# Conditioning rows in PSUM, a narrower first stage and twice the load buffers in a diffusion layer

## The chip, the cores and the metric

The kernel runs on one core of a Trainium2 chip. The metric is the device time of one execution, in microseconds (us). The kernel before took 854.05 us (median of 3 runs, 852.78 to 855.21). Lower is better.

## The reference, cut to what matters

One layer of a diffusion backbone over 512 latent tokens with 256 context tokens, all in float32, width 1024:

```python
mod   = silu(c) @ w_ada + b_ada          # six vectors of 1024: sh1, sc1, g1, sh2, sc2, g2
mod_c = silu(c_ctx) @ w_ada + b_ada      # the same for the context; only sh1c, sc1c are used
uc = layer_norm(ctx) * (1 + sc1c) + sh1c
kvc = uc @ w_in[:, :KV_COLS]             # context keys and values -> start states of the scans
u = layer_norm(x) * (1 + sc1) + sh1
k, v, q, g, p_in, gate_a, gate_b = split(u @ w_in)
ret  = retention(q, k, v, g, states) @ w_branch_ret     # 8 heads, forward and backward, swish gate g
pool = pool_mixer(p_in) @ w_branch_pool                 # means over windows of 2, 4, 8, 16
mix  = (sigmoid(gate_a) * ret + sigmoid(gate_b) * pool) @ w_out
x = layer_norm(ALPHA * x + g1 * mix) * ln1_g + ln1_b
u2 = layer_norm(x) * (1 + sc2) + sh2
x = layer_norm(ALPHA * x + g2 * conv_ffn(u2)) * ln2_g + ln2_b
```

`conv_ffn` is an up-projection to 2 x 2816, a 3x3 depthwise convolution, gelu times gate and a down-projection.

## The kernel before, in words

Every large product is done in three passes of 128x512 matmuls on operands that are split in a rounded high part and the rest: hi x hi, hi x lo, lo x hi. `split` (L84) makes the two parts of a weight tile: ScalarE (ACT) casts `raw` to `hi` (L88), and GpSimd (POOL) or VectorE (DVE) subtracts to get `lo` (`sub`, L83). The tiles `hi` and `lo` have two buffers each, the landing tile `raw` has three (L63). PSUM has eight banks, handed out by `bank()`.

The latent tokens lie feature-major: 8 tiles kt of 128 features x 512 tokens (`xnT`, after the norm and a transpose). The first stage goes over kt = 0 to 7. For each kt it loads two blocks of `w_ada` (512 KB each; `wst`) and one of `w_first` (`first_load`), the columns of q (4 tiles of 128) and of the first N_G0 = 4 swish gate tiles. `first_mod` gets the shift and the scale of this kt: `matvec` (L201) multiplies a 128x1024 block by `silu_c`, a row that stands in SBUF on all partitions (made by `silu_row`, L107), and sums along the row, and `finish_mod` (L204) adds the bias, for a scale also the 1. `modulate` (L212) then forms `uh` (ACT, L214) and, by way of `u` (ACT, L217), `ul` (POOL, L83). TensorE (PE) multiplies: `g0_mm` (L334) does hi, lo and ul passes for the four q tiles and then for the four gate tiles, which fill all eight banks over the whole stage. From kt = 4 on, `ctx_mod` (L222) makes the same shift and scale for the context, two blocks per kt, with `silu_cc` in SBUF (L225).

After it come steps of one weight tile each (`step`, `run_steps`, L171): step i first preloads and splits the weights of step i + 1 (`prep`), then multiplies and does what its `post` says. In this order: four gate steps `g_step` for the other four gate tiles (with q's copies from PSUM, L410, the statistics, transposes and modulation of the context, and the rest of `ctx_mod`), the pool step `p_step(0)`, four key steps (`kv_steps`), `p_step(1)`, eight value steps with `p_step(2)` and `p_step(3)` among them, then eight steps each for the two branch gates, during which the retention is done, and the two branch projections (L742, L754). Each key and value step also loads three more 512 KB blocks of `w_ada` by way of `raw` and multiplies them on DVE (`ada_tiles`). The table of decays (`decay_tables`) is made in the first key step: ACT does 16 exponentials of 128x128 (L559, L560) in a row.

What sets the order: within `ordered(*ORDS)` all engines do their instructions in the order of the code. The first stage stands in such a region. After it the kernel calls `ordered(*ORD0)`, which keeps only PE, SP (the queue that issues all DMAs) and DVE in the order of the code, and from the first key step on only SP is kept; what isn't kept is put in order by a scheduler that works with times of its own. The output projection (L804 on), the up-projection with its convolution (L1020 on) and the down-projection follow.

Of the kernel before, what the change touches and what calls it, by code (L numbers as in the profile page):

```python
# [9 lines left out]
F32 = mybir.dt.float32  # L10
# [19 lines left out]
ALPHA = 2.0 ** 0.25  # L30
N_G0 = 4
N_FRONT = 18
# [13 lines left out]
def layer_kernel(ctx: ExitStack, tc: tile.TileContext, a: dict):  # L46
# [16 lines left out]
    def raw4(shape=(P, D)):  # L63
        return sb.tile(list(shape), F32, tag="raw", bufs=3, name=nm("raw"))

    def row():
        return sb.tile([P, D], F32, tag="row", bufs=3, name=nm("row"))
# [33 lines left out]
    mod = keep("mod", [P, 48])  # L101
    modc = keep("modc", [P, 16])
    neg_half = keep("neg_half", [P, 1])
    dve.memset(neg_half, -0.5)
    keep("gap0", [P, 24])

    def silu_row(cols):  # L107

        t = row()
        for hf in range(2):  # L110
            ps = bank()
            for j in range(4):
                k = 4 * hf + j
                pe.transpose(ps[:, j * P:(j + 1) * P], cols[:, k:k + 1].broadcast_to([P, P]), ident)
            act.copy(t[:, hf * SEQ:(hf + 1) * SEQ], ps)
        return t

# [85 lines left out]

    def finish_mod(m, j, scale):  # L204
        dve.tensor_scalar(m[:, j:j + 1], m[:, j:j + 1], bada[:, j:j + 1], 1.0 if scale else 0.0, ALU.add, ALU.add)

# [15 lines left out]
    def ctx_mod(kt):  # L222
        for j in (kt, 8 + kt):
            w = ada_slot(j)
            dve.scalar_tensor_tensor(w, w, 1.0, silu_cc, ALU.mult, ALU.mult, accum_out=modc[:, j:j + 1])  # L225
            finish_mod(modc, j, j >= 8)

# [13 lines left out]
    def first_load(kt):  # L241
        for j in (kt, 8 + kt):
            load(ada_slot(j), a["wada"][j])
        return load(raw4((P, NF0)), a["w_first"][kt])

    def first_mod(kt):
        for j in (kt, 8 + kt):
            matvec(j, ada_slot(j), junk)
            finish_mod(mod, j, j >= 8)

# [44 lines left out]
    dve.tensor_tensor(cols[:, 1], cols[:, 0], cols[:, 1], ALU.mult)  # L295
    silu_c = silu_row(cols[:, 1])
    x_stats(1)
# [13 lines left out]
    held = [x_trans(0, 1)]  # L311
    matvec(0, ada_slot(0), junk)
    x_norm(3, dve, lo_half)
# [4 lines left out]
    warm(N_W)  # L318
    finish_mod(mod, 0, False)
    matvec(8, ada_slot(8), junk)  # L320
    finish_mod(mod, 8, True)
    wh, wl = (sb.tile([P, NF0], F32R, tag=t, bufs=2, name=nm(t)) for t in ("hi", "lo"))
    act.activation(uh[:, 0, :], xnT[:, 0, :], AF.Identity, bias=mod[:, 0:1], scale=mod[:, 8:9])
    for cs, cp in ((lo_half, dve.tensor_copy), (hi_half, act.copy)):
        cp(wh[:, cs], raw0[:, cs])
        sub(pool, wl[:, cs], raw0[:, cs], wh[:, cs].bitcast(F32))
# [14 lines left out]
    for kt in range(NKT):  # L341
        wh, wl = ready
        if kt == 0:
            g0 = [bank() for _ in range(4)]
            g0_mm(kt, range(0, 4), range(2))
            held += [x_trans(2, 1), x_trans(3, 1)]
            g0_mm(kt, range(0, 4), range(2, 3))
            for h in held:
                act.copy(*h)
            g0 += [bank() for _ in range(N_G0)]  # L350
            ready = split(first_load(1), (P, NF0), pool)
            first_mod(1)
            modulate(mod, 1, 9, xnT[:, 1, :], uh[:, 1, :], ul[:, 1, :], pool)
        elif kt + 1 < NKT:
            ready = first_prep(kt + 1, first_load(kt + 1))
        if kt:
            g0_mm(kt, range(0, 4))
        g0_mm(kt, range(4, 4 + N_G0))
        if kt == 1:
            silu_cc = load(row(), a["c_ctx"].broadcast_to([P, D]))  # L360
        elif kt == 2:
            for hf in range(2):
                cs = slice(hf * SEQ, (hf + 1) * SEQ)
                t = t2()
                act.activation(t, silu_cc[:, cs], AF.Sigmoid)
                dve.tensor_tensor(silu_cc[:, cs], silu_cc[:, cs], t, ALU.mult)
# [29 lines left out]

    def ctx_trans():
        for tb in range(2):
            transpose_tb(put_ctxT, ctx_raw[:, tb, :], tb)

    def ctx_modulate():
        for kt in range(NKT):
            modulate(modc, kt, 8 + kt, ctx_nT[:, kt, :], uch[:, kt, :], ucl[:, kt, :], pool,
                     act if kt % 2 else dve)

    def g_step(h):
        def post(ps):
            if h == N_G0:
                for f in range(4):
                    act.activation(qT[:, f, :], g0[f], AF.Copy, scale=DK ** -0.5)  # L410
                for f in range(2):
# [3 lines left out]
                for tb, (mu, rs) in enumerate(ctx_stats):
                    dve.tensor_scalar(ctx_raw[:, tb, :], ctx_raw[:, tb, :], mu, rs, ALU.subtract, ALU.mult)
            elif h == N_G0 + 1:
                for f in range(2, N_G0):
                    put_g(f, g0[4 + f])
                ctx_mod(h)  # L420
            elif h == N_G0 + 2:
                ctx_trans()
                ctx_mod(h)
# [107 lines left out]
    def decay_tables():  # L531
# [29 lines left out]
        for g in range(2):
            t = t2((P, 4, P))
            for j in range(4):
                h = 4 * g + j
                dve.tensor_scalar(t[:, j, :], grids[:, 0, :], lgf[:, h:h + 1], None, ALU.mult)
                dve.scalar_tensor_tensor(t[:, j, :], grids[:, 1, :], lgb[:, h:h + 1], t[:, j, :], ALU.mult, ALU.add)
            act.activation(t, t, AF.Exp)
            dve.tensor_tensor(kv[2][:, 4 * g:4 * g + 4, :], t, ident.unsqueeze(1).broadcast_to([P, 4, P]), ALU.add)

# [677 lines left out]
```

## Time and profile before

| what | value |
|---|---|
| median of 3 runs | 854.05 us |
| the profiled execution, its own time | 853.42 us |
| its span, first to last instruction | 851.6 us |
| PE busy | 810.9 us (95%) |
| DVE, POOL, ACT busy | 568.0, 422.1, 360.6 us |
| mean granted clock of PE | 0.99 |
| moved by DMA | 106.94 MB |

PE is busy for 95% of the span, so what can be had lies in the 41 us in which it isn't, and in the few stretches with a lower granted clock. The page's slices show where they are: at the start, in slices 2 to 4, 6 and 9 of 40 (the first stage and the key and value steps), around the output projection, and behind PE's last matmul.

### The profile page before, as it was taken

How to read it: one execution, taken by the hardware profiler on the slowest of the kernel's cores; microseconds unless marked ns; L12 is line 12 of the kernel's file. 1: busy time of each engine (PE TensorE's matmuls, PEld its weight loads, DVE VectorE, ACT ScalarE, POOL GpSimd, SP SyncE). 2: the span in 40 equal slices, each digit the busy share in tenths (PEclk: the TensorE clock that was granted, in tenths of full speed). 3: DMA queues.
4: the chain of work that ended last, by engine and by line, in shares of the span. 5: the costliest groups of instructions: out<-in, count | busy, mean ns of one | idle time of the engine just before them, and what ended most of it. 6: DMA issues, size and time to landing. Idle time of an engine off the chain costs nothing.

```text
span 851.6 us, 10522 instructions
## 1 busy us (share of the span) xinstructions
PE 810.9 (95%) x3865; PEld 673.7 (79%) x3865; DVE 568.0 (67%) x967; ACT 360.6 (42%) x574; POOL 422.1 (50%) x301
## 2 busy tenths in 40 slices
PE   6988999989999999999899899999999999999993
PEld 4767877868788888888687898888888888888883
DVE  7899996777247774253756759888877777512148
ACT  4434636131354323233414557666666666223200
POOL 4876420303353213022633768988888888211245
PEclk9999999999999999999999999999999999999997
DMA  9932357677311103234613511332222323333202
GB/s 353 347 120 76 124 197 237 212 246 239 104 50 50 50 25 125 99 124 163 205 64 123 174 38 64 123 99 94 93 90 97 100 99 99 108 111 130 73 1 99
DMA packets 33780, 106.94 MB, mean 126 GB/s; under 512 B 4528, under 2 KB 5312, under 8 KB 33728
## 3 DMA queue, kind: packets, MB, share of 16 engines
q1 hardware_dynamic: 33728, 106.27, 36.7%
q8 instruction: 30, 0.49, 0.2%
q14 instruction: 22, 0.18, 0.1%
HBM read 104.14 MB, written 2.11 MB: 125 GB/s over the span
## 4 chain that ended last, share of the span: by engine, by line
PE 43%; DVE 3%; POOL 2%; ACT 1%; issue 1%; POOLq 0%; DVEq 0%
PE ps L95 14%; PE ps L94 14%; PE ps L93 14%; POOL S L83 1%; ACT t L871 1%; DVE S L1140 1%; DVE S L1149 1%; DVE S L835 1%; DVE sm L836 0%; POOL sm L123 0%; DVE xr L848 0%; DVE t L1135 0%; POOL sm L122 0%; POOL S L1147 0%; POOL S L1117 0%
## 5 line engine op out<-in xcount | busy, mean ns | idle before, releaser
L95 PE MATMUL ps<-S,lo 128*128 128x512 f32 (+1 forms) x544 | 210.3, 388 | 5.0 <-POOL lo L83 2.6
L93 PE MATMUL ps<-S,hi 128*128 128x512 f32 (+1 forms) x544 | 211.4, 389 | 2.6 <-ACT hi L88 2.6
L94 PE MATMUL ps<-S,hi 128*128 128x512 f32 (+1 forms) x544 | 210.6, 387 | 0.0
L83 POOL TENSOR_TENSOR lo<-raw,hi 128x1024 fp32r<-128x1024 f32 (+1 forms) x63 | 147.7, 2346 | 124.0 <-ACT hi L88 112.9
L965 DVE SCALAR_TENSOR_TENSOR t<-ps,convw,t 128x441 f32<-128x441 f32 (+1 forms) x258 | 163.8, 691 | 45.7 <-POOL t L963 45.5
L88 ACT CAST hi<-raw 128x1024 fp32r<-128x1024 f32 (+1 forms) x98 | 99.4, 1014 | 161.8 <-PE ps L94 52.3
L95 PEld LDWEIGHTS ps<-S,lo 128*128 128x128 f32 x544 | 102.7, 189 | 27.5 <-POOL lo L83 3.5
L93 PEld LDWEIGHTS ps<-S,hi 128*128 128x128 f32 x544 | 102.2, 188 | 23.4 <-ACT hi L88 3.0
L963 POOL TENSOR_TENSOR t<-t,t 128x448 f32<-128x448 f32 x88 | 101.9, 1158 | 36.0 <-ACT t L1046 32.5
L94 PEld LDWEIGHTS ps<-S,hi 128*128 128x128 f32 x544 | 102.4, 188 | 20.3
L94 PE MATMUL ps<-S,S 128*128 128x512 f32 (+1 forms) x308 | 112.2, 364 | 0.0
L95 PE MATMUL ps<-S,S 128*128 128x512 f32 (+1 forms) x308 | 112.2, 364 | 0.0
L93 PE MATMUL ps<-S,S 128*128 128x512 f32 (+1 forms) x308 | 111.4, 365 | 0.0
L83 DVE TENSOR_TENSOR lo<-raw,hi 128x1024 fp32r<-128x1024 f32 x37 | 51.0, 1379 | 49.4 <-ACT hi L88 49.3
L94 PE MATMUL ps<-lo,S 128*128 128x512 f32 x208 | 81.3, 391 | 0.9 <-DVE lo L83 0.9
L95 PE MATMUL ps<-hi,S 128*128 128x512 f32 x208 | 80.8, 389 | 0.0
L83 POOL TENSOR_TENSOR S<-raw,S 128x1024 fp32r<-128x1024 f32 x21 | 50.4, 2402 | 59.9 <-ACT S L734 44.4
L93 PE MATMUL ps<-hi,S 128*128 128x512 f32 x208 | 77.5, 391 | 0.0
L1043 ACT ACTIVATE t<-ps,convb,convw 128x512 f32<-128x512 f32 x43 | 33.6, 780 | 76.2 <-PE ps L95 76.2
L93 PEld LDWEIGHTS ps<-S,S 128*128 128x128 f32 x308 | 58.1, 189 | 9.2
L95 PEld LDWEIGHTS ps<-S,S 128*128 128x128 f32 x308 | 58.1, 189 | 9.2
L94 PEld LDWEIGHTS ps<-S,S 128*128 128x128 f32 x308 | 58.1, 189 | 9.1
(208 smaller groups left out, 1130.2 us busy)
## 6 DMA issues: line engine op xcount, KB each, us to landing
raw<-in_w_up SPq DMA_DIRECT2D x44, 512.0 KB, 3.3
raw<-in_wada SPq DMA_DIRECT2D x32, 512.0 KB, 4.0
raw<-in_w_down SPq DMA_DIRECT2D x22, 512.0 KB, 3.3
S<-in_wada SPq DMA_DIRECT2D x16, 512.0 KB, 6.8
raw<-in_w_first SPq DMA_DIRECT2D x8, 512.0 KB, 7.7
raw<-in_w_v SPq DMA_DIRECT2D x16, 256.0 KB, 3.0
raw<-in_w_ga SPq DMA_DIRECT2D x8, 512.0 KB, 3.4
raw<-in_w_gb SPq DMA_DIRECT2D x8, 512.0 KB, 3.3
```

The lines of the kernel that those rows point to most:

```text
L83: eng.tensor_tensor(out, x, y, ALU.subtract)
L88: act.copy(hi, raw)
L93: pe.matmul(out, lhsT=sh, rhs=mh, start=first, stop=False)
L94: pe.matmul(out, lhsT=sh, rhs=ml, start=False, stop=False)
L95: pe.matmul(out, lhsT=sl, rhs=mh, start=False, stop=last)
L835: dve.scalar_tensor_tensor(z, ps, rs, lnb[:, cs], ALU.mult, ALU.add)
L871: act.activation(u[:, j, :], ps[:, js], AF.Identity, bias=sh, scale=sc)
L963: pool.tensor_tensor(o, o, i, ALU.add)
L965: dve.scalar_tensor_tensor(o, i, w, o, ALU.mult, ALU.add)
L1043: act.activation(acc, src, AF.Identity, bias=convb[:, i:i + 1], scale=convw[:, i, 4:5])
L1140: dve.scalar_tensor_tensor(z, z, mu, lng, ALU.subtract, ALU.mult)
L1149: dve.scalar_tensor_tensor(z, z, scale[tb], lnb[:, cs], ALU.mult, ALU.add)
```

## The change

Five things are edited. (1) `silu_row` also hands back the two PSUM banks in which the conditioning row was built, and `first_matvec` multiplies by these in two halves of 512, with a second accumulator `part`; likewise for the context, where `ctx_mod` uses `silu_ch`, two banks. (2) N_G0 goes from 4 to 2: the first stage does 6 column tiles per kt instead of 8, `w_first` shrinks from 512 to 384 KB per kt, and there are six gate steps instead of four. (3) The context products leave the first stage, but for the first pair, and go one pair to a gate step; the context's norm, transposes and modulation are spread over the gate steps and the first two pool steps; `p_step(1)` moves ahead of the key steps. (4) `raw` gets six buffers. (5) The 1 of the scales is added once to the bias, and the decay table is made in four pieces over four steps. The call `ordered(*ORD0)` behind the first stage goes away, and q's copies move ahead of the steps.

```diff
-N_G0 = 4
+N_G0 = 2
...
-        return sb.tile(list(shape), F32, tag="raw", bufs=3, name=nm("raw"))
+        return sb.tile(list(shape), F32, tag="raw", bufs=6, name=nm("raw"))
...
+    part = keep("part", [P, 2, 16])
...
+    def matvec2(m, p2, j, w, halves):
+
+        for hf, dst in enumerate((m, p2)):
+            cs = slice(hf * SEQ, (hf + 1) * SEQ)
+            dve.scalar_tensor_tensor(w[:, cs], w[:, cs], 1.0, halves[hf], ALU.mult, ALU.mult,
+                                     accum_out=dst[:, j:j + 1])
+        dve.tensor_scalar(m[:, j:j + 1], m[:, j:j + 1], p2[:, j:j + 1], bada[:, j:j + 1], ALU.add, ALU.add)
...
     def ctx_mod(kt):
         for j in (kt, 8 + kt):
-            w = ada_slot(j)
-            dve.scalar_tensor_tensor(w, w, 1.0, silu_cc, ALU.mult, ALU.mult, accum_out=modc[:, j:j + 1])
-            finish_mod(modc, j, j >= 8)
+            matvec2(modc, part[:, 1], j, ada_slot(j), silu_ch)
...
     def first_mod(kt):
         for j in (kt, 8 + kt):
-            matvec(j, ada_slot(j), junk)
-            finish_mod(mod, j, j >= 8)
+            first_matvec(j)
...
         if kt >= 6:
             load(ctx_raw[:, kt - 6, :], a["ctx"][(kt - 6) * P:(kt - 5) * P, :])
-        if kt >= 4:
-            ctx_mod(kt - 4)
-    ordered(*ORD0)
+        if kt == NKT - 2:
+            silu_ch = [bank() for _ in range(2)]
+            for hf in range(2):
+                dve.tensor_tensor(silu_ch[hf], silu_cc[:, hf * SEQ:(hf + 1) * SEQ], gate_c[hf], ALU.mult)
+            ctx_mod(0)
 
     qk = slot(0, [P, 2, 4, SEQ])
     qT, kT = qk[:, 0], qk[:, 1]
+    for f in range(4):
+        act.activation(qT[:, f, :], g0[f], AF.Copy, scale=DK ** -0.5)
...
     def g_step(h):
         def post(ps):
...
+            n = h - N_G0
+            if n in (1, 2):
+                ctx_norm(n - 1)
+            if n == 0:
+                ctx_mod(1)
+                for f in range(N_G0):
                     put_g(f, g0[4 + f])
...
             else:
-                ctx_mod(h)
-                ctx_modulate()
+                ctx_mod(n + 1)
             put_g(h, ps)
+            if n in (3, 4):
+                transpose_tb(put_ctxT, ctx_raw[:, n - 3, :], n - 3)
+            elif n == 5:
+                ctx_modulate(0)
+                ctx_modulate(1)
...
+        for g in range(2):
+            defer(1 + g, table_rows, grids, g)
+            defer(3 + g, table_mask, grids, g)
...
     p_step(0)
+    p_step(1)
     steps_k = len(steps)
     kv_steps(a["w_k"], True, k_post)
-    p_step(1)
```

`first_matvec` is `matvec2` with `silu_h`, `mod` and an output that is thrown away.

On DVE, the products of kt = 6 in the first stage before, and the context pair in front of them (S is a block of `w_ada`, `mod` and `modc` the sums, `row` a conditioning row in SBUF):

```order
L225 SCALAR_TENSOR_TENSOR S_2_71,modc<-S_2_71,row_318 128x1024
L205 TENSOR_SCALAR modc<-modc,bada 128x1
L225 SCALAR_TENSOR_TENSOR S_2_71,modc<-S_2_71,row_318 128x1024
L205 TENSOR_SCALAR modc<-modc,bada 128x1
L202 SCALAR_TENSOR_TENSOR S_1_70,mod<-S_5_74,row_110 128x1024
L205 TENSOR_SCALAR mod<-mod,bada 128x1
L202 SCALAR_TENSOR_TENSOR S_1_70,mod<-S_5_74,row_110 128x1024
L205 TENSOR_SCALAR mod<-mod,bada 128x1
```

And in the changed kernel, at the same kt (`ps` are the two banks of the row, `part` the sum of the second half):

```order
L258 SCALAR_TENSOR_TENSOR S_1_71,mod<-S_5_75,ps_112 128x512
L258 SCALAR_TENSOR_TENSOR S_1_71,part<-S_5_75,ps_118 128x512
L260 TENSOR_SCALAR mod<-mod,part,bada 128x1
L258 SCALAR_TENSOR_TENSOR S_1_71,mod<-S_5_75,ps_112 128x512
L258 SCALAR_TENSOR_TENSOR S_1_71,part<-S_5_75,ps_118 128x512
L260 TENSOR_SCALAR mod<-mod,part,bada 128x1
```

The context's products no longer stand between those of the latent tokens, and one product is now two instructions of half the width with one input in PSUM.

On ACT, the passage from the first stage to the gate steps before (hi_498 is the last tile of `w_first`, hi_585 the first of `w_g`; L410 are q's copies out of PSUM):

```order
L88 CAST hi_498<-raw_496 128x1024
L214 ACTIVATE S_8_77<-S_7_76,mod 128x512
L217 ACTIVATE t_79_507<-S_7_76,mod 128x512
L88 CAST hi_585<-raw_583 128x1024
L410 ACTIVATE S_80_571<-ps_216 128x512
L410 ACTIVATE S_80_571<-ps_217 128x512
L410 ACTIVATE S_80_571<-ps_218 128x512
L410 ACTIVATE S_80_571<-ps_219 128x512
```

And in the changed kernel (L392 are q's copies, hi_547 and hi_553 the first two tiles of `w_g`):

```order
L392 ACTIVATE S_80_529<-ps_226 128x512
L88 CAST hi_547<-raw_545 128x1024
L88 CAST hi_553<-raw_551 128x1024
L397 ACTIVATE t_93_588<-ps_251 128x512
L397 ACTIVATE t_94_591<-ps_252 128x512
L397 ACTIVATE t_95_594<-ps_557 128x512
```

The first row is the last of the four copies: the cast of the first gate step's weights, which the scheduler had put ahead of the copies, now stands behind all four.

## Rows read from the trace of the kernel before

**Rows 1.** PE's waits over the whole span: total us, times, longest.

```profile
PE ps L338 <- ACT S L214: 4.7, 3, 2.2
PE ps L95 <- POOL lo L83: 2.6, 2, 2.1
PE ps L93 <- ACT hi L88: 2.6, 1, 2.6
PE ps L95 <- DVE lo L83: 2.4, 1, 2.4
PE ps L94 <- DVE lo L83: 0.9, 2, 0.5
```

**Rows 2.** The timeline of PE: start us, us, instruction, idle before.

```profile
23.31 1.98 PE L338 MATMUL ps<-S,hi 128*128 128x512 f32 x8
29.94 1.98 PE L338 MATMUL ps<-S,hi 128*128 128x512 f32 x8
31.75 1.07 PE L338 MATMUL ps<-S,lo 128*128 128x512 f32 x4
69.29 2.14 PE L338 MATMUL ps<-S,hi 128*128 128x512 f32 x8 [0.70 <-POOL S L83]
73.09 0.39 PE L93 MATMUL ps<-S,hi 128*128 128x512 f32 x1
```

**Rows 3.** The timeline of DVE and POOL in the first stage.

```profile
19.87 1.21 DVE L202 SCALAR_TENSOR_TENSOR S<-S,row 128x1024 f32<-128x1024 f32 x1
...
58.56 1.22 DVE L225 SCALAR_TENSOR_TENSOR S<-S,row 128x1024 f32<-128x1024 f32 x1
58.89 2.02 POOL L83 TENSOR_TENSOR S<-t,S 128x512 fp32r<-128x512 f32 x1 [2.98 <-ACT t L217]
59.95 2.04 DVE L202 SCALAR_TENSOR_TENSOR S<-S,row 128x1024 f32<-128x1024 f32 x1
60.88 3.37 POOL L83 TENSOR_TENSOR lo<-raw,hi 128x1024 fp32r<-128x1024 f32 x1
62.17 3.16 DVE L202 SCALAR_TENSOR_TENSOR S<-S,row 128x1024 f32<-128x1024 f32 x1
```

**Rows 4.** Single lines on DVE: duration min/median/max in ns.

```profile
L965 DVE SCALAR_TENSOR_TENSOR t<-ps,convw,t x258: 662/671/743, 501.0 to 726.7; 128x441 f32<-128x441 f32 x86, 128x504 f32<-128x504 f32 x43
L820 DVE SCALAR_TENSOR_TENSOR ps<-xr,ps x8: 695/696/697, 431.7 to 474.2; 128x512 f32<-128x512 f32 x8
L205 DVE TENSOR_SCALAR modc<-modc,bada x16: 214/214/217, 48.2 to 97.9; 128x1 f32<-128x1 f32 x16
```

**Rows 5.** ACT and POOL at the passage to the gate steps, and a short POOL row.

```profile
35.93 1.30 POOL L83 TENSOR_TENSOR S<-t,S 128x512 fp32r<-128x512 f32 x1
69.83 2.07 ACT L410 ACTIVATE S<-ps 128x512 f32<-128x512 f32 x4 [1.75 <-PE ps L338]
73.58 1.05 ACT L88 CAST hi<-raw 128x1024 fp32r<-128x1024 f32 x1
74.71 2.40 POOL L83 TENSOR_TENSOR lo<-raw,hi 128x1024 fp32r<-128x1024 f32 x1 [2.13 <-ACT hi L88]
```

**Rows 6.** Windows of 10 us: busy of PE, PEld, DVE, ACT, POOL, granted clock, DMA share, GB/s.

```profile
20.00:30.00 10.00, 9.11 (x44) 7.27 (x43) 9.86 (x13) 6.12 (x8) 7.59 (x3) 1.00 1.00 402
40.00:50.00 10.00, 7.65 (x26) 5.36 (x26) 9.82 (x16) 3.98 (x5) 5.64 (x3) 0.83 0.62 227
130.00:140.00 10.00, 10.00 (x39) 8.04 (x38) 8.31 (x16) 5.39 (x10) 0.14 (x2) 0.83 0.75 228
180.00:190.00 10.00, 7.62 (x34) 5.96 (x33) 8.18 (x13) 3.79 (x5) 0.39 (x1) 1.00 0.78 237
```

**Rows 7.** ACT and SP in the key and value steps.

```profile
128.43 1.03 ACT L88 CAST hi<-raw 128x1024 fp32r<-128x1024 f32 x1
183.10 1.05 ACT L88 CAST hi<-raw 128x1024 fp32r<-128x1024 f32 x1 [3.17 <-DMA raw<-in_w_v]
178.68 0.80 SPq L98 DMA_DIRECT2D raw<-in_w_v  x2
```

More of the change, by code (lines that the diff above doesn't have):

```diff
@@ L109, in silu_row @@
         t = row()
+        halves = []
         for hf in range(2):
             ps = bank()
+            halves.append(ps)
             for j in range(4):
@@ L115, in silu_row @@
             act.copy(t[:, hf * SEQ:(hf + 1) * SEQ], ps)
-        return t
+        return t, halves
     def ln_scale(st):
@@ L202, in matvec, with finish_mod @@
         dve.scalar_tensor_tensor(out_junk, raw, 1.0, silu_c, ALU.mult, ALU.mult, accum_out=mod[:, j:j + 1])
-    def finish_mod(m, j, scale):
-        dve.tensor_scalar(m[:, j:j + 1], m[:, j:j + 1], bada[:, j:j + 1], 1.0 if scale else 0.0, ALU.add, ALU.add)
+    def matvec2(m, p2, j, w, halves):
[4 more added lines that the diff above has]
+        dve.tensor_scalar(m[:, j:j + 1], m[:, j:j + 1], p2[:, j:j + 1], bada[:, j:j + 1], ALU.add, ALU.add)
+    def finish_mod(m, j):
+        dve.tensor_scalar(m[:, j:j + 1], m[:, j:j + 1], bada[:, j:j + 1], None, ALU.add)
     xs = slot(0, [P, NTB, D])
@@ L244, in first_load, with first_matvec @@
         return load(raw4((P, NF0)), a["w_first"][kt])
+    def first_matvec(j):
+        for hf, dst in enumerate((mod, part[:, 0])):
+            cs = slice(hf * SEQ, (hf + 1) * SEQ)
+            dve.scalar_tensor_tensor(junk[:, cs], ada_slot(j)[:, cs], 1.0, silu_h[hf], ALU.mult, ALU.mult,
+                                     accum_out=dst[:, j:j + 1])
+        dve.tensor_scalar(mod[:, j:j + 1], mod[:, j:j + 1], part[:, 0, j:j + 1], bada[:, j:j + 1],
+                          ALU.add, ALU.add)
     def first_mod(kt):
         for j in (kt, 8 + kt):
-            matvec(j, ada_slot(j), junk)
-            finish_mod(mod, j, j >= 8)
+            first_matvec(j)
     def first_prep(kt, raw):
@@ L295, in layer_kernel @@
     dve.tensor_tensor(cols[:, 1], cols[:, 0], cols[:, 1], ALU.mult)
-    silu_c = silu_row(cols[:, 1])
+    silu_c, silu_h = silu_row(cols[:, 1])
     x_stats(1)
@@ L311, in layer_kernel @@
     held = [x_trans(0, 1)]
-    matvec(0, ada_slot(0), junk)
+    for j in (8, 32):
+        dve.tensor_scalar(bada[:, j:j + 8], bada[:, j:j + 8], 1.0, None, ALU.add)
+    first_matvec(0)
     x_norm(3, dve, lo_half)
@@ L318, in layer_kernel @@
     warm(N_W)
-    finish_mod(mod, 0, False)
-    matvec(8, ada_slot(8), junk)
-    finish_mod(mod, 8, True)
+    first_matvec(8)
     wh, wl = (sb.tile([P, NF0], F32R, tag=t, bufs=2, name=nm(t)) for t in ("hi", "lo"))
     act.activation(uh[:, 0, :], xnT[:, 0, :], AF.Identity, bias=mod[:, 0:1], scale=mod[:, 8:9])
-    for cs, cp in ((lo_half, dve.tensor_copy), (hi_half, act.copy)):
+    for cs, cp in ((lo_half, dve.tensor_copy), (slice(SEQ, NF0), act.copy)):
         cp(wh[:, cs], raw0[:, cs])
@@ L332, in layer_kernel @@
     ready = wh, wl
+    for h in held:
+        act.copy(*h)
     def g0_mm(kt, fs, passes=range(3)):
@@ L345, in layer_kernel @@
             g0_mm(kt, range(0, 4), range(2))
-            held += [x_trans(2, 1), x_trans(3, 1)]
+            held = [x_trans(2, 1), x_trans(3, 1)]
             g0_mm(kt, range(0, 4), range(2, 3))
@@ L350, in layer_kernel @@
             g0 += [bank() for _ in range(N_G0)]
-            ready = split(first_load(1), (P, NF0), pool)
-            first_mod(1)
-            modulate(mod, 1, 9, xnT[:, 1, :], uh[:, 1, :], ul[:, 1, :], pool)
+            ready = first_prep(1, first_load(1))
         elif kt + 1 < NKT:
@@ L358, in layer_kernel @@
         g0_mm(kt, range(4, 4 + N_G0))
-        if kt == 1:
+        if kt == 3:
             silu_cc = load(row(), a["c_ctx"].broadcast_to([P, D]))
-        elif kt == 2:
+        elif kt == 5:
+            gate_c = [t2() for _ in range(2)]
             for hf in range(2):
[L363 to L366, printed above, removed]
+                act.activation(gate_c[hf], silu_cc[:, hf * SEQ:(hf + 1) * SEQ], AF.Sigmoid)
         if kt >= 6:
             load(ctx_raw[:, kt - 6, :], a["ctx"][(kt - 6) * P:(kt - 5) * P, :])
-        if kt >= 4:
-            ctx_mod(kt - 4)
-    ordered(*ORD0)
+        if kt == NKT - 2:
[3 more added lines that the diff above has]
+            ctx_mod(0)
     qk = slot(0, [P, 2, 4, SEQ])
     qT, kT = qk[:, 0], qk[:, 1]
+    for f in range(4):
+        act.activation(qT[:, f, :], g0[f], AF.Copy, scale=DK ** -0.5)
     gs = slot(7, [P, H, SEQ])
@@ L389, in feature_step @@
         step(lambda wh, wl: post(feature_mm(wh, wl, nkt, mh, ml)), src, (P, nkt, P), eng)
-    uc = slot(5, [P, 2, NKT, CTX], F32R)
+    uc = slot(1, [P, 2, NKT, CTX], F32R)
     uch, ucl = uc[:, 0], uc[:, 1]
@@ L395, in put_ctxT, with ctx_modulate, ctx_norm @@
         act.copy(ctx_nT[:, g * 4:(g + 1) * 4, tb * P:(tb + 1) * P], ps)
[L397 to L404, printed above, removed]
+    def ctx_modulate(kt):
+        modulate(modc, kt, 8 + kt, ctx_nT[:, kt, :], uch[:, kt, :], ucl[:, kt, :], pool,
+                 act if kt % 2 else dve)
+    def ctx_norm(tb):
+        mu, rs = ln_stats(ctx_raw[:, tb, :])
+        nmr = small([P, 1])
+        dve.tensor_scalar(nmr, mu, rs, -1.0, ALU.mult, ALU.mult)
+        act.activation(ctx_raw[:, tb, :], ctx_raw[:, tb, :], AF.Identity, bias=nmr, scale=rs)
     def g_step(h):
         def post(ps):
[L408 to L411, printed above, removed]
-                    put_g(f, g0[4 + f])
-                ctx_stats = [ln_stats(ctx_raw[:, tb, :]) for tb in range(2)]
-                ctx_mod(h)
[L415 to L423, printed above, removed]
-            else:
-                ctx_mod(h)
-                ctx_modulate()
+            n = h - N_G0
[4 more added lines that the diff above has]
+                for f in range(N_G0):
+                    put_g(f, g0[4 + f])
+            else:
+                ctx_mod(n + 1)
             put_g(h, ps)
+            if n in (3, 4):
[3 more added lines that the diff above has]
+                ctx_modulate(1)
         feature_step(a["w_g"][h - N_G0], NKT, uh, ul, post, pool)
@@ L438, in ada_tiles @@
                 matvec(j, raw, raw)
-                finish_mod(mod, j, 32 <= j < 40)
+                finish_mod(mod, j)
     poolT = slot(8, [P, 2, 4, SEQ], F32R)
@@ L445, in post @@
         def post(ps):
+            if gi == 0:
+                ctx_mod(7)
+            if gi < 2:
+                for kt in range(2 + 3 * gi, 5 + 3 * gi):
+                    ctx_modulate(kt)
             invc = load(t2(), a["invc"][gi:gi + 1, :].broadcast_to([P, SEQ]))
@@ L557, in decay_tables, with table_rows, table_mask @@
         tabs[1] = eb_t.rearrange("p (h c) -> p h c", h=H)
-        for h in range(H):
+        for g in range(2):
+            defer(1 + g, table_rows, grids, g)
+            defer(3 + g, table_mask, grids, g)
+    def table_rows(grids, g):
+        for h in range(4 * g, 4 * g + 4):
             act.activation(tabs[0][:, h, :], grids[:, 2, :], AF.Exp, scale=lgf[:, h:h + 1])
             act.activation(tabs[1][:, h, :], grids[:, 3, :], AF.Exp, scale=lgb[:, h:h + 1])
[L561 to L568, printed above, removed]
+    def table_mask(grids, g):
+        t = t2((P, 4, P))
+        for j in range(4):
+            h = 4 * g + j
+            dve.tensor_scalar(t[:, j, :], grids[:, 0, :], lgf[:, h:h + 1], None, ALU.mult)
+            dve.scalar_tensor_tensor(t[:, j, :], grids[:, 1, :], lgb[:, h:h + 1], t[:, j, :], ALU.mult, ALU.add)
+        act.activation(t, t, AF.Exp)
+        dve.tensor_tensor(kv[2][:, 4 * g:4 * g + 4, :], t, ident.unsqueeze(1).broadcast_to([P, 4, P]), ALU.add)
     v = slot(6, [P, NTB, D])
@@ L1235 @@
     host.update(_constants())
-    nc = _bacc.Bacc("TRN2", target_bir_lowering=False, num_devices=1)
+    nc = _bacc.Bacc("TRN2", target_bir_lowering=False, num_devices=1, dynamic_dma_scratch_size=1024)
     arrays, aps = {}, {}
```

## The prediction, made before the changed kernel ran

> **What bounds the kernel now.** I read the page's busy shares first: PE is busy for 95% of the span, so its matmuls, whose number the change leaves as it is, set some 811 us, and only its waits and its clock can be gained or lost. PE's waits [rows 1] put them in three places. In the first stage it waits for `uh` and `ul` (4.7 us for ACT L214 alone), in the key and value steps for `hi` and `lo` (2.6, 2.4 and 0.9 us), and later for a POOL `lo` in the second branch projection (2.6 us).
>
> The first stage next. Matmuls of 512 columns start 0.226 us apart: eight and then the next four stand 1.81 us apart [rows 2]. At kt = 1 and later a kt has 24, so it needs 5.44 us. The second half of the eight at 23.31 belongs to kt = 1, which so begins at 24.2, and the first gate step begins at 73.09 [rows 2]: 48.9 us for 7 x 5.44 = 38.1 us of work. 10.8 us are lost here, to waits and to a slow clock.
>
> What holds it is DVE, which is busy for 9.8 of 10 us [rows 6], and the rows say why. A product of 128x1024 takes 1.22 us, and the next starts 1.39 us after it (58.56 to 59.95), its sum and bias included [rows 3]. But the one at 59.95 takes 2.04 us and the one at 62.17 takes 3.16 us, and each ends about 1.1 us behind the end of a POOL subtraction (at 60.91 and 64.25). POOL's 1024 subtraction in turn is called 3.37 us long where it takes 2.40 us alone [rows 3, 5]. So a DVE instruction that reads two tensors in SBUF and a POOL subtraction take turns, whole instructions at a time. With four products to a kt, 4 x 1.39 + 1.30 + 2.40 = 9.3 us, with two 6.5 us, both above PE's 5.44 us.
>
> **The change part by part.** *The product with a PSUM row.* The trace has no such instruction. The nearest rows are two: L820 reads one tensor in SBUF and one in PSUM, 512 wide, in 0.70 us at its longest, and L965, which writes to SBUF while POOL is busy beside it, takes 0.66 to 0.74 us in all 258 cases [rows 4]. None shows the 1 to 2 us of a turn. What follows a product adds 1.39 - 1.22 = 0.17 us [rows 3]; I charge it to each half: 2 x (0.70 + 0.17) = 1.7 us a product, 3.4 us a kt. At best it is the old 1.39 us, at worst a blocked 3.16 us; I take the value of the rows of the same form.
>
> [...]
>
> *Six tiles to a kt.* PE now needs 18 x 0.226 = 4.08 us a kt. POOL: the `ul` subtraction at 1.30 us and one of 768 columns, between 1.30 and 2.40 us, about 1.85, so 3.2 us. ACT was busy 6.1 of 10 us with wider casts [rows 6] and isn't the bound. DVE 3.4 us. All are below 4.08, so PE leads. DMA must bring 1.44 MB a kt; at the 402 GB/s of [rows 6] that is 3.6 us; 2.1 MB of x, 11.5 MB of weights and 0.5 MB of the context's row take 35 us, so the tiles of kt = 7 land near 40 us, ahead of their cast.
>
> So: kt = 0 has six matmuls fewer and ends at 24.2 - 1.36 = 22.8, and about 0.4 later, since its two products cost 0.3 us more each, the first of them partly beside a wait of DVE. The products of kt = 1 can't start before 19.87 [rows 3], where DVE is done with the norms; with 3.4 us and 0.8 us for `uh` on ACT (the 1024 cast has 1.05 [rows 5]) PE gets it at 24.1, a wait of 1.3 us behind 22.8. Then 0.8 us for `u` and 1.30 us on POOL make `ul` 0.5 us later than the eight matmuls before it. From there seven times 4.08: the stage ends at T = 22.8 + 0.4 + 1.8 + 28.6 = 53.6. The matmuls that go to the gate steps, 48 x 0.226 = 10.9, have to be added: 64.5 against 73.1, **8.6 us gained**. If PE never waited, 10.4; if DVE needed 4.5 us a kt, 7 x 0.4 less, 5.7.
>
> *The passage to the gate steps.* Before, the cast of the first gate weights stood ahead of q's copies on ACT, and PE went from the stage into the gate steps without a wait. Now all four copies stand in front of it. They follow the last pass of the q tiles: the first copy starts 0.54 us behind that pass's first matmul (69.29 to 69.83) and all take 2.07 us [rows 2, 5]. In the changed kernel that pass starts ten matmuls before the end, at T - 2.3, so the copies end at T + 0.35, the cast of 1.05 us at T + 1.4, the subtraction of 2.40 us on POOL at T + 3.9 [rows 5]. PE waits 1.4 us for `hi`, does two matmuls, waits 2.0 us more for `lo`: **3.5 us lost**, a new wait. Behind the cast stand the second cast and the swish of the gates, which nobody awaits so early. Its bounds are 0 (if the copies were done early) and 4.5 us (if POOL's subtraction has to take a turn with DVE, 1 us).
>
> [...]
>
> *The context's work in the gate steps.* One step has 24 matmuls, 5.44 us. ACT's swish (q's copies, of the same width, stand 0.5 us apart [rows 5]), the cast and POOL's subtraction need 0.6 + 1.05 + 2.40, and in steps 1 and 2 a norm of 1024 columns on ACT comes on top, over the 1.05 us of a cast, say 1.3: 5.4 us, which just fits, since `lo` is wanted 0.45 us into a step. DVE's two products and a swish, 4.1 us, fit as well. I take 0 here, with 4 us as a bound. In the two pool steps POOL has eight context subtractions (256 wide, 0.7 us each as half of 1.30 [rows 5]) and seven window operations of 1.3 us, about 15 us, and the DVE splits of the keys have two SBUF inputs and so take turns with them, as in [rows 3]: **1.0 us lost** at the first key step, between 0 and 3.
>
> *Six buffers and the decay table.* The cast at 128.43 came behind ACT's 16 exponentials, and PE waited 2.6 us for it; the one at 183.10 waited 3.17 us for a load that SP could issue only at 178.68, when one of three buffers came free [rows 7]. With six buffers the load of the next tile no longer needs those of the three blocks of `w_ada` just ahead of it, so it can start a step earlier (a step is 36 matmuls, 8.1 us), and the exponentials come later and stand in front of a cast that is not due yet. 2.6 + 2.4 + 0.9 [rows 1] and the 1.7 us of clock behind 130 [rows 6] should go: **7.6 us gained**; at least 0, if the loads find another stall. What is late next is PE itself.
>
> *The rest.* The bias with its 1, the shorter `finish`, the moved loads of SP lie beside PE's work: 0. In the second branch projection POOL's order changes (two output weights in a row ahead of the third `lo`); the wait of 2.6 us [rows 1] may move by 1.5 us either way; I take 0. Everything behind it is the same.
>
> Sum: -8.6 + 3.5 + 0.9 + 1.0 - 7.6 = -10.8. The profiled execution took 853.4 us, so 842.6; the median of the runs lies 0.6 above it: **843.2 us**.
>
> **The rivals.** *The waits of the key and value steps stay* (12%): the buffers move a wait to the next load or to DVE, which in the traced order makes products before it makes `lo`. DVE's 8.2 to 8.3 busy us of 10 there [rows 6] speak for it, the row of the late load against it [rows 7]. 843.2 + 7.6 = 850.8.
>
> *The gate steps become bound by the ACT, POOL chain* (12%): 5.4 us of 5.44 leaves nothing; a miss of 1 us in each of five steps gives 848.
>
> *More goes* (10%): the wait of the second projection too, and the clock holds: 843.2 - 2.6 - 0.9 = 839.7.
>
> *The turns stay* (5%), the slower side: if the halves still waited for POOL, a kt would take 3.4 + 3.2 = 6.6 us on DVE and POOL together, above 4.08, and the stage would lose 7 x 2.5 = 17 instead of 1.8, so 8.6 gained becomes 7 lost, 858.6. The point from which it decides is 4.08 us a kt. Against it stand all 258 rows of L965. [...]
>
> **How the numbers follow.** The forecast has 61%, with 840 to 847 as its own range. The range of 838.5 to 851 takes in the three faster rivals, the first at its edge, and leaves out the turns and some tails. A change under 0.3% (2.6 us) can't be told from none by a measurement of this kernel; faster by more 0.92, within 0.03 (a quarter of the first rival, which ends near that line), slower 0.05.
>
> **What would show it.** Right: products of about 0.7 us a half with none above 1 us in the first stage, PE without waits from kt = 2 on and its first gate matmul near 55; then a wait for `hi` of some 1.4 us and for `lo` of some 2 us; no wait over 1 us between 110 and 220. Wrong: halves of 1.5 us or more, a PE that waits for ACT L214 in each kt, a wait in each gate step, a cast that waits for `w_v`.

## The result and the profile after

The changed kernel took 845.65 us (median of 5 runs, 845.12 to 849.95) beside 854.87 us for the kernel before in the same session: ratio 0.9904, 95% interval 0.9884 to 0.9925. A second session gave 846.06 us and 0.9897 (0.9870 to 0.9923). By the first ratio the gain is 8.2 us; 10.8 were forecast. The profiled execution took 847.08 us against 853.42, 6.3 us less. One run of the last combination below took 908.41 us at a granted clock of 0.85 and is left out of its figures.

PE's waits in the changed kernel (engine and line, what it waited for: us in all, times, the longest), to be read beside [rows 1]; those of the start and of the output projection are left out:

```profile
PE ps L95 <- POOL lo L83: 4.6, 2, 2.9
PE ps L93 <- ACT hi L88: 1.7, 2, 1.0
PE ps L95 <- DVE lo L83: 1.0, 1, 1.0
PE ps L93 <- ACT S L546: 1.0, 2, 0.5
PE ps L356 <- ACT S L225: 0.9, 1, 0.9
```

The 4.7 us for `uh` are down to 0.9. PE still waits for `lo`, but in other places (the passage, the first key step, the second projection), and the waits for the key copies L546 are new. The first stage around kt = 1 (start, length, engine, line, operation; in brackets the idle time before and what ended it) answers to [rows 2, 3]:

```profile
21.86 1.83 POOL L83 TENSOR_TENSOR lo<-raw,hi 128x768 fp32r<-128x768 f32 x1 [3.71 <-ACT hi L88]
22.58 0.68 DVE L258 SCALAR_TENSOR_TENSOR S<-S,ps 128x512 f32<-128x512 f32 x1
23.56 1.20 PE L356 MATMUL ps<-S,hi 128*128 128x512 f32 x4 [0.86 <-ACT S L225]
24.30 1.30 POOL L83 TENSOR_TENSOR S<-t,S 128x512 fp32r<-128x512 f32 x1 [0.61 <-ACT t L228]
```

The halves take 0.68 us with POOL busy beside them (0.675 to 0.689 in all 32 of the stage), and POOL's subtractions take 1.83 and 1.30 us: no turns. PE waits once at kt = 1. The passage to the gate steps:

```profile
50.27 1.52 PE L356 MATMUL ps<-S,hi 128*128 128x512 f32 x6
50.69 2.07 ACT L392 ACTIVATE S<-ps 128x512 f32<-128x512 f32 x4 [3.81 <-PE ps L356]
52.08 0.61 PE L356 MATMUL ps<-S,hi 128*128 128x512 f32 x2
52.62 2.01 ACT L88 CAST hi<-raw 128x1024 fp32r<-128x1024 f32 x2
53.74 0.50 PE L93 MATMUL ps<-S,hi 128*128 128x512 f32 x1 [1.04 <-ACT hi L88]
56.18 0.80 PE L95 MATMUL ps<-S,lo 128*128 128x512 f32 x1 [1.71 <-POOL lo L83]
```

The stage's last matmul starts at 52.31 and the next could start 0.23 us later, so the stage is over at 52.5. Then q's copies stand in front of the cast on ACT, and PE waits 1.04 and 1.71 us as the profile lists it. A listed wait is somewhat short: a matmul is listed 0.39 us long, though the next one can start 0.23 us behind it. By the starts, PE loses 1.2 us (52.54 to 53.74) and 1.9 us (54.30 to 56.18). The windows (us; length; busy time of PE, PEld, DVE, ACT, POOL; granted clock; DMA share, GB/s), beside [rows 6]:

```profile
50.00:60.00 10.00, 7.25 (x24) 5.23 (x24) 3.05 (x8) 4.93 (x8) 4.69 (x2) 0.83 0.22 69
110.00:120.00 10.00, 9.62 (x43) 7.64 (x41) 6.58 (x17) 3.18 (x4) 7.62 (x9) 1.00 0.73 240
120.00:130.00 10.00, 9.36 (x41) 7.72 (x42) 9.97 (x28) 2.17 (x4) 0.00 (x0) 1.00 0.98 367
130.00:140.00 10.00, 8.84 (x39) 6.76 (x37) 9.89 (x31) 8.32 (x26) 0.14 (x2) 1.00 0.97 331
140.00:150.00 10.00, 9.50 (x34) 7.43 (x35) 10.00 (x22) 7.37 (x18) 0.00 (x0) 0.83 0.87 287
180.00:190.00 10.00, 10.00 (x45) 8.28 (x45) 8.21 (x12) 2.58 (x3) 7.75 (x5) 1.00 0.47 159
400.00:410.00 10.00, 9.29 (x34) 7.60 (x35) 4.44 (x7) 3.69 (x6) 6.81 (x5) 0.83 0.60 219
```

The wait of 180 to 190 is gone. But PE loses 1.0 us in 110 to 130, 1.7 us in 130 to 150, and the clock falls behind the passage, behind 141 and behind 401 (0.83 over 10 us is 1.7 us lost). What stands before the loss at 138 to 141:

```profile
131.68 0.30 ACT L569 ACTIVATE kdec<-lg,pcols 128x8 f32<-128x8 f32 x1 [3.50 <-DVE lg L568]
136.97 0.39 ACT L584 ACTIVATE row<-t,lg 128x128 f32<-128x128 f32 x1
137.83 1.03 ACT L88 CAST hi<-raw 128x1024 fp32r<-128x1024 f32 x1
138.91 0.50 PE L93 MATMUL ps<-hi,S 128*128 128x512 f32 x1 [0.66 <-ACT hi L88]
139.29 0.56 ACT L546 COPY S<-ps 128x512 f32<-128x512 f32 x1
139.91 0.50 PE L93 MATMUL ps<-hi,S 128*128 128x512 f32 x1 [0.50 <-ACT S L546]
140.28 1.54 ACT L546 COPY S<-ps 128x512 f32<-128x512 f32 x3
140.91 0.50 PE L93 MATMUL ps<-hi,S 128*128 128x512 f32 x1 [0.50 <-ACT S L546]
```

The table was to be made in pieces, but all 16 exponentials still run in a row behind `lg`, from 132.57 to 137.4. The first value weight's cast and the key copies queue behind them, and the first value step wants the weight and the banks that these copies free.

### The profile page after: what moved, and what is told of

The parts are those of the page before. It is cut to its first block, busy times and chain, and to the rows that moved or that the text cites. A ratio compares the mean times of both kernels' runs of the same rounds, so it can differ in the third digit from the quotient of the medians.

```text
span 845.3 us, 10601 instructions
## 1 busy us (share of the span) xinstructions
PE 811.7 (96%) x3865; PEld 676.7 (80%) x3865; DVE 545.3 (65%) x1033; ACT 363.3 (43%) x578; POOL 405.8 (48%) x303
## 4 chain that ended last, share of the span: by engine, by line
PE 82%; DVE 7%; POOL 4%; ACT 3%; issue 2%; DMA 1%; SPq 0%; POOLq 0%; DVEq 0%
PE ps L95 24%; PE ps L94 24%; PE ps L93 24%; PE ps L356 3%; POOL S L83 2%; PE ps L632 1%; PE ps L668 1%; PE ps L669 1%; PE ps L638 1%; ACT t L896 1%; PE ps L635 1%; DVE raw L205 1%; DVE lo L83 1%; DMA S<-in_x 1%; PE ps L298 1%
## 5 line engine op out<-in xcount | busy, mean ns | idle before, releaser
L95 PE MATMUL ps<-S,lo 128*128 128x512 f32 (+1 forms) x560 | 217.4, 390 | 5.6 <-POOL lo L83 4.6
L93 PE MATMUL ps<-S,hi 128*128 128x512 f32 (+1 forms) x560 | 218.6, 390 | 1.0 <-ACT hi L88 1.0
L94 PE MATMUL ps<-S,hi 128*128 128x512 f32 (+1 forms) x560 | 217.4, 388 | 0.0
L83 POOL TENSOR_TENSOR lo<-raw,hi 128x1024 fp32r<-128x1024 f32 (+2 forms) x65 | 141.1, 2172 | 158.5 <-ACT hi L88 155.6
L88 ACT CAST hi<-raw 128x1024 fp32r<-128x1024 f32 (+2 forms) x100 | 100.0, 1001 | 181.5 <-PE ps L95 67.7
L95 PEld LDWEIGHTS ps<-S,lo 128*128 128x128 f32 x560 | 106.0, 189 | 28.6 <-POOL lo L83 5.4
L93 PEld LDWEIGHTS ps<-S,hi 128*128 128x128 f32 x560 | 106.1, 189 | 22.6 <-ACT hi L88 1.5
L94 PEld LDWEIGHTS ps<-S,hi 128*128 128x128 f32 x560 | 106.0, 189 | 21.1
```

The lines of the kernel that those rows point to most:

```text
L83: eng.tensor_tensor(out, x, y, ALU.subtract)
L88: act.copy(hi, raw)
L93: pe.matmul(out, lhsT=sh, rhs=mh, start=first, stop=False)
L94: pe.matmul(out, lhsT=sh, rhs=ml, start=False, stop=False)
L95: pe.matmul(out, lhsT=sl, rhs=mh, start=False, stop=last)
```

## The experiments

Gains by ratio are taken on 854.9 us for the kernel before.

**Copies behind the cast.** In `run_steps`, q's copies are emitted behind the first weight's split:

```
-    for f in range(4):
-        act.activation(qT[:, f, :], g0[f], AF.Copy, scale=DK ** -0.5)
...
         ready = prep(0)
+        q_copies()
```

Expected: 

> The changed kernel, but ACT makes the first gate step's weight cast ahead of q's four copies. Theory (the program order on ACT makes PE wait at the passage, and the granted clock falls because of that wait): PE's waits of 1.2 us for hi and 2.0 us for lo behind 53 us go, and so does the stretch at half clock behind 56 us, 1.7 us: 4.9 us less than the changed kernel, 840.8 us by medians. Rival 1 (the clock falls there for another reason): only 3.2 us less, 842.4 us. Rival 2 (the first gate step then waits for a bank that q's copies free late, so the wait only moves): 845.7 us, with a wait of 2 to 3 us for an ACT copy in the same place.

Measured: 842.45 us, ratio 0.9849 (0.9823 to 0.9876), 4.7 us less than the changed kernel. The same window now has no wait and the full clock:

```profile
50.00:60.00 10.00, 10.00 (x45) 8.26 (x44) 4.25 (x11) 5.63 (x9) 4.85 (x3) 1.00 0.36 107
```

So the wait comes from ACT's program order, and no wait for a bank takes its place. Whether the 1.7 us of clock are part of the gain can't be told from the times: the interval is 4.5 us wide and holds the 4.9 us of the theory and the 3.2 us of rival 1.

**The row in SBUF.** `first_matvec` becomes `matvec(j, ada_slot(j), junk)` and `finish_mod(mod, j)`, one product of 1024 columns.

Expected: 

> The changed kernel, but the products of the first stage read the conditioning row from SBUF, one product of 1024 columns instead of two halves from PSUM. Theory (a DVE instruction with two inputs in SBUF and a POOL subtraction take turns): products of 1.2 us and of 2 us and more, up to 3.2 us, DVE 2.8 us and POOL 3.2 us one behind the other, 6.0 us a kt against 4.08 us of PE, seven times 1.9: about 13 us more than the changed kernel, 859 us, slower than the kernel before. Rival (the narrower stage alone makes the gain, PE's work shrinks and 2.8 us of DVE fit beside POOL): within 1 us of 845.7 us.

Measured: 851.44 us, ratio 0.9959 (0.9940 to 0.9978), 4.7 us more than the changed kernel, where the theory had 13. One kt of its first stage:

```profile
36.16 2.83 POOL L83 TENSOR_TENSOR lo<-raw,hi 128x768 fp32r<-128x768 f32 x1
36.26 1.66 PE L352 MATMUL ps<-S,hi 128*128 128x512 f32 x6 [0.62 <-POOL S L83]
37.46 2.62 DVE L205 SCALAR_TENSOR_TENSOR S<-S,row 128x1024 f32<-128x1024 f32 x1
39.18 2.04 POOL L83 TENSOR_TENSOR S<-t,S 128x512 fp32r<-128x512 f32 x1 [0.18 <-ACT t L228]
40.25 2.04 DVE L205 SCALAR_TENSOR_TENSOR S<-S,row 128x1024 f32<-128x1024 f32 x1
41.27 1.66 PE L352 MATMUL ps<-S,hi 128*128 128x512 f32 x6 [0.61 <-POOL S L83]
```

The turns are there: DVE's and POOL's intervals overlap, but each end lies 1.1 to 1.7 us behind the other engine's end, an instruction's own length. The kt lasts 5.01 us (36.26 to 41.27) and not 6.0: I had summed 2 x 1.39 + 3.15. The `tensor_scalar` behind each product costs nothing there, since it lies beside POOL's turn (0.21 us at 37.33, under POOL's row of 36.16), so 2 x 1.22 + 1.85 + 1.30 = 5.59, and each of the four changes of turn overlaps by another 0.14. The mechanism holds; a turn costs less than I charged. With POOL busy beside it, a product of 1024 columns with both inputs in SBUF takes 2.04 to 2.62 us here, and each half with one input in PSUM takes 0.68 us in the changed kernel.

**Six buffers alone, in the kernel before:** `bufs=3` to `bufs=6` for `raw`, and the smaller DMA scratch.

Expected: 

> The kernel before with six load buffers instead of three and nothing else (the DMA scratch is cut to make room, as in the changed kernel). Theory (the buffers end the waits of the key and value steps): the wait for the late load near 183 us (2.4 and 0.9 us) goes, and the 2.6 us behind the exponentials near 128 us with its 1.7 us of clock too, since the cast is due before them: 7.6 us less, 847.3 us. Rival 1 (the exponentials still stand in front of the cast, since nothing spreads them): only 3.3 us less, 851.6 us. Rival 2 (the buffers do nothing, the late load waits for something else): 854.9 us.

Measured: 848.83 us, ratio 0.9920 (0.9891 to 0.9948), 6.8 us less than before. Between 80 and 250 us this is PE's only wait, and the exponentials are still in front of the cast:

```profile
PE ps L95 <- DVE lo L83: 0.6, 1, 0.6
126.68 0.39 ACT L560 ACTIVATE row<-t,lg 128x128 f32<-128x128 f32 x1
126.97 1.04 ACT L88 CAST hi<-raw 128x1024 fp32r<-128x1024 f32 x1
```

The cast at 126.97 is no longer awaited. One number gives about four fifths of the whole gain, and the 3.3 us of rival 1 lie outside the interval (4.4 to 9.3 us). But the cast doesn't come early, and the exponentials don't come later: they start 1.5 us sooner than before (122.29 instead of 123.75), and PE is ready 1.0 us later (127.79 instead of 126.79). The cast ends at 128.01 and PE starts at 128.06, so the wait of 2.6 us went by a narrow margin.

**Three buffers in the changed kernel:** `bufs=6` back to `bufs=3`.

Expected: 

> The changed kernel with three load buffers instead of six. Theory: a load of the value weights is issued late again, 3.3 us more than the changed kernel (849 us), and up to 7.6 us more if the cast behind the exponentials is late too. Rival (the six gate steps and the spread tables did it, the buffers nothing): within 1 us of 845.7 us.

Measured: 856.22 us, ratio 1.0013 (0.9996 to 1.0031): everything else in the change together gains nothing without the buffers. It is 9.3 us more than the changed kernel. This run keeps the smaller DMA scratch, an edit of the change that the list of five leaves out, so the 9.3 us are due to the buffers alone. PE loses 2.5 us and 3.4 us of clock in one window and 4.1 us in another:

```profile
140.00:150.00 10.00, 7.46 (x19) 5.27 (x20) 9.08 (x25) 9.63 (x22) 0.00 (x0) 0.66 0.77 240
180.00:190.00 10.00, 5.92 (x25) 4.64 (x25) 5.11 (x8) 2.58 (x3) 3.19 (x2) 0.97 0.58 199
```

The kernel before lost 7.5 us between 110 and 220, this one 14.6: what the first stage gains is lost again here.

**The pool step between keys and values.** `p_step(1)` goes back behind the key steps, and its three context modulations into `p_step(0)`:

```
     p_step(0)
-    p_step(1)
     steps_k = len(steps)
     kv_steps(a["w_k"], True, k_post)
+    p_step(1)
```

Expected: 

> The changed kernel with the second pool step back between the key and the value steps, as before; all context modulation that stood in it goes into the first pool step. Theory A (the value steps stand directly behind the key steps, so they ask for banks and a weight before ACT is done with its exponentials and the key copies): the wait of 1.7 us at 138 to 140 and the 1.7 us of slow clock behind it go, 3.4 us less than the changed kernel, 842.3 us by medians. Theory B (the exponentials in a row are the cause, wherever the step stands): the waits stay or come elsewhere in the key steps, 845.7 us or within 1 us of it.

Measured: 841.66 us, ratio 0.9853 (0.9827 to 0.9880), 4.4 us less than the changed kernel, 1.0 more than theory A had. PE has no wait between 110 and 220 us; the one at 119.5 went as well.

**The table behind the keys:**

```
     def decay_tables():
-        kv_bufs()
...
-    queue.setdefault(steps_k, []).append((decay_tables, ()))
+    queue.setdefault(steps_k, []).append((kv_bufs, ()))
+    queue.setdefault(steps_k + 4, []).append((decay_tables, ()))
```

Expected: 

> The changed kernel with the whole decay table, its load and its exponentials begun four steps later, in the first value step, so that ACT makes the key copies ahead of the exponentials; the value steps stay directly behind the key steps. Theory B (ACT's order is the cause): the wait of 1.7 us at 138 to 140 with its 1.7 us of clock goes, and the 1.0 us at 119.5 us too, since the load of the decay grid no longer stands ahead of a load of the key weights on SP: 4.4 us less than the changed kernel, 841.3 us. Theory A (a value step needs six banks while six are still full, whatever ACT's order): 1 to 3 us of waits for the key copies stay, 844 to 845.7 us.

Measured: 841.71 us, ratio 0.9838 (0.9812 to 0.9865), 5.6 us less than the changed kernel. No wait is left between 100 and 220 us; ACT makes copies and cast as soon as the key sums are there:

```profile
133.66 2.63 ACT L546 COPY S<-ps 128x512 f32<-128x512 f32 x4 [3.21 <-PE ps L95]
137.54 1.05 ACT L88 CAST hi<-raw 128x1024 fp32r<-128x1024 f32 x1
```

Either edit alone removes the whole loss, so neither theory is the cause by itself: the value steps directly behind the key steps and the exponentials in front of the copies are both needed for it.

**The second projection:** `BP_W` from (0, 0, 3, 3) to (0, 1, 3, 5) for the output blocks, and POOL in the order of the code (`ORDB` with `E_POOL`).

Expected: 

> The changed kernel with POOL kept in the order of the code in the second branch projection, and the four output weight blocks made in its steps 0, 1, 3 and 5 instead of 0, 0, 3 and 3. Theory (two subtractions of 1024 columns in a row stand in front of a weight's lo): PE's wait of 2.9 us near 400 us and the 1.7 us of slow clock behind it go, 4.6 us less than the changed kernel, 841.1 us. Rival (the output weights come late by this and the output projection waits instead): within 1 us of 845.7 us, or slower by up to 3 us.

Measured: 843.76 us, ratio 0.9870 (0.9846 to 0.9893), 2.9 us less. First the changed kernel, where two subtractions stand ahead of `lo`, then this one:

```profile
393.71 5.72 POOL L83 TENSOR_TENSOR S<-row,S 128x1024 fp32r<-128x1024 f32 x2
400.71 0.80 PE L95 MATMUL ps<-S,lo 128*128 128x512 f32 x1 [2.87 <-POOL lo L83]
```

```profile
393.84 2.40 POOL L83 TENSOR_TENSOR S<-row,S 128x1024 fp32r<-128x1024 f32 x1 [0.66 <-POOL lo L83]
398.51 0.50 PE L95 MATMUL ps<-S,lo 128*128 128x512 f32 x1 [1.24 <-POOL lo L83]
```

One POOL subtraction fewer ahead of `lo` was worth over half of the wait. 1.24 us stay: one such subtraction (393.84) still stands ahead, and the one that makes this `lo`, at 396.19, takes 2.26 us beside a DVE subtraction with two inputs in SBUF (394.74 to 397.32), where the next `lo` takes 1.29: a turn again. That the turn makes 1.0 of the 1.24 us is worked out from these rows; no run takes it away alone.

**Three buffers with the pool step between:** both edits above on the changed kernel.

Expected: 

> The changed kernel with three load buffers and with the second pool step back between the key and the value steps. With three buffers and the value steps directly behind the key steps the kernel took 856.2 us, 14 us of waits and slow clock between 110 and 220 us against 7.5 us in the kernel before. Theory (the pool step without a block of the conditioning weights gives the three buffers time to be freed, so the move of that step is what made three buffers worse): 5 to 8 us less, 848 to 851 us. Rival (the wait comes from other edits, the spread tables or the gate steps): 855 to 857 us.

Measured: 851.67 us, ratio 0.9968 (0.9941 to 0.9996), 3.8 us less than with three buffers alone, below the 5 to 8 expected. Moving the step explains part of why three buffers got worse; the single runs lie from 847.6 to 857.1, too wide to divide the rest.

**The combinations.** Copies behind the cast and the table behind the keys; and these with the second projection, its output blocks in steps 1, 2, 4 and 6.

Expected of the two: 

> The changed kernel with two edits together, q's copies behind the first gate weight's cast and the decay table begun in the first value step; the second projection as in the changed kernel. Theory (the gains add up): 8.2 + 4.7 + 5.6 = 18.5 us less than the kernel before, 836.4 us, with the wait of 2.9 us near 390 us left. Rival (they share a gain): 838 to 841 us.

Measured: 836.29 us, ratio 0.9779 (0.9751 to 0.9807).

Expected of the three: 

> The changed kernel with three edits together: q's copies behind the first gate weight's cast, the decay table begun in the first value step, and the second projection with POOL in the order of the code and its output blocks in steps 1, 2, 4 and 6. Theory (the three waits stand in different places and add up): against the kernel before 8.2 us of the change, 4.7 us of the copies, 5.6 us of the table and 2.9 us of the projection, 21.4 us in all: 833.5 us, and no wait of PE over 1.3 us between 30 and 430 us. Rival (part of it moves to the next wait, the output projection above all): 836 to 839 us.

Measured: 833.50 us, ratio 0.9746 (0.9720 to 0.9773), the fastest, 20.8 to 21.7 us less than before. The gains add up, as far as the intervals tell (18.9 us by ratio for the two, where 18.5 were expected; 21.7 for the three, where 21.4 were). PE's longest waits that are left behind the start (L892 is the output projection, which nothing here touched, and L357 the first stage at kt = 1):

```profile
PE ps L892 <- issue: 2.1, 1, 2.1
PE ps L892 <- ACT xr L881: 0.9, 1, 0.9
PE ps L357 <- ACT S L226: 0.9, 1, 0.9
PE ps L95 <- POOL lo L83: 0.6, 1, 0.6
```

The changed kernel beside them, expected: 

> The changed kernel itself once more, beside the two that combine the edits: 845.7 us and a ratio of 0.990 to the kernel before; with the clock falling behind the same waits in some executions and not in others, single runs spread by 2 to 5 us.

Measured: 846.06 us, ratio 0.9897 (0.9870 to 0.9923), single runs from 843.9 to 849.4.

## Why the prediction was nearly right, and which terms failed

The time fell into the range and the direction held, in part by luck: 10.8 us were forecast, 8.2 measured by the ratio and 6.3 found between the two profiled executions, and errors of opposite sign met in the sum. The sizes below are taken from the starts of PE's matmuls in the two profiled executions, since listed waits are short.

- *First stage, -8.6.* It was more: T is 52.5, not 53.6, which makes 9.7 gained. Halves of 0.68 us and a kt of 4.08 us without waits from kt = 2 on are as forecast; the wait at kt = 1 was 0.86 us as listed, 1.0 by the starts, where 1.3 was charged, since the first product of kt = 1 began at 19.54, before the 19.87 that I took as its earliest time. With the row in SBUF the stage ends 5.7 us later (58.2), so that much is the PSUM row's; the other 4.0 us come from the narrower stage and from the context's products that left it, which no run separates.
- *Passage, +3.5.* 1.2 + 1.9 = 3.1 us: the mechanism and both waits are there, and taking q's copies out of the way removes them.
- *Clock, +0.9.* No run shows this term: 1.7 us here, and over all profiles with this passage 0, 1.7 or 3.4 us, 1.3 on average (see the last section), so it was too low a price. And I charged it once: in the profiled execution the clock fell at four places, the passage, behind 141, behind 401 (0.83 in each of the three windows) and in the output projection (0.91 over 470 to 490).
- *First key step, +1.0.* 1.3 us lost, listed as 1.02, and the charged cause is only half of it:

```profile
111.36 0.33 SPq L98 DMA_DIRECT2D t<-in_grids  x1
111.75 0.89 SPq L98 DMA_DIRECT2D raw<-in_w_k  x2
116.69 1.79 DVE L83 TENSOR_TENSOR t<-t,t 128x512 fp32r<-128x512 f32 x1
116.85 1.05 ACT L88 CAST hi<-raw 128x1024 fp32r<-128x1024 f32 x1 [1.93 <-DMA raw<-in_w_k]
120.64 0.50 PE L95 MATMUL ps<-S,lo 128*128 128x512 f32 x1 [1.02 <-DVE lo L83]
```

  The cast waited 1.93 us for `w_k`, whose load SP issued behind the load of the decay grid, and that one had stood 7.7 us until POOL's context subtractions freed its tile. Then DVE's turn with POOL (1.79 us, where the same form takes 0.69 at 124.73) held up `lo`, which began at 119.36 though its cast had ended at 117.9. Begun four steps later, the table's load left no wait; that `lo` would have come in time without the turn as well is worked out from these rows and was not run.
- *Key and value steps, -7.6.* **This term failed:** it is -5.0. The old waits did go, and the six buffers alone took them away: 6.8 us in the kernel before. What was wrong is the sentence that PE itself is late next. I took the table's four pieces to be spread, because the code defers them; the scheduler put them together behind a late `lg`, so that they did come later, as I had reasoned, but in front of a cast that was due. And I charged nothing for the second pool step's move, which set the value steps directly behind the key copies. Together they cost 4.1 us, 2.4 of waits (1.66 as listed) and 1.7 of clock: PE's lead over the kernel before falls there from 8.2 us (its 501st matmul) to 4.1 (its 576th).
- *The rest, 0.* It is +2.4. The second projection's wait went from 2.6 to 2.9 us, inside the 1.5 allowed, but now in one piece, and the clock fell behind it (0.83; 1.00 there in the execution before): +1.5. In the output projection the waits shrank by 0.5 us and the clock fell once (0.91 over 470 to 490, 1.00 before): +0.9.

Summed, -9.7 + 3.1 + 1.7 + 1.3 - 5.0 + 2.4 = -6.2 of the 6.3 us between the two profiled executions. The later terms are read from PE's progress. Both kernels do 3865 matmuls, and the 276th, 851st, 1901st and 2301st start at 81.02, 218.76, 425.12 and 497.73 us before and at 76.16, 210.20, 418.07 and 491.51 after: a lead of 4.9 us behind the passage, 8.6 behind the value steps, 7.05 behind the second projection and 6.2 behind the output projection.

Of the rivals, the waits of the key and value steps came back in half their size by another mechanism; the gate steps had no wait in 60 to 110; the turns did not stay, and would have cost 5.01 us a kt rather than 6.6.

## What to carry to other kernels

When loads come late, count the buffers first: one pool's depth alone gave 6.8 of the 8.2 us. The rest of the change gave nothing clear of the noise, with three buffers or with six, not because its arithmetic failed (the first stage gained 9.7 us) but because new waits behind it took the gain back; without two of these the whole is worth 18.9 us. Where a loop ends, look at what stands in front of the next loop's first weight cast on its engine; where a scheduler orders an engine, a deferred call is no promise, so read the order it made. Before moving a filler step, ask which copies it gave time to.

## What the runs showed of the hardware

The same wait in the same place is followed by a slow clock in one execution and not in the next. The passage costs PE the same 2.75 us in each of these three (the changed kernel again, the pool step between, three buffers with the pool step between), the granted clock differs:

```profile
50.00:60.00 10.00, 7.25 (x31) 5.35 (x30) 3.04 (x8) 4.93 (x8) 4.70 (x2) 1.00 0.22 63
```

```profile
50.00:60.00 10.00, 7.25 (x31) 5.36 (x30) 3.04 (x8) 4.92 (x8) 4.71 (x2) 1.00 0.22 74
```

```profile
50.00:60.00 10.00, 7.25 (x22) 5.18 (x21) 2.45 (x7) 4.92 (x8) 4.70 (x2) 0.75 0.27 88
```

The first is the very kernel that had 0.83 there in its first profile. Eight profiles have this passage with its two waits. Behind it the clock fell in five of them: once in four (0.83 over one window in three of them, 0.89 and 0.94 over two in the fourth), which costs 1.7 us, and twice in the third above (0.75 here and 0.91 in the next window), which costs 3.4. So the price beside the wait's own length was 0 to 3.4 us, 1.3 on average. In the three profiles in which q's copies stand behind the cast there is no wait and the clock is 1.00.
